# Two phased K pairs instead of four in the second chunk pair, and rests made by adding transfers

## The chip, the cores and the metric

The kernel runs on one core of a Trainium2 chip, as one program. Its time is the device time in microseconds. The core has five engines that run their own streams of instructions and wait for one another by semaphores: TensorE (PE, matrix products), VectorE (DVE), ScalarE (ACT), GpSimd (POOL) and SyncE (SP), which here only issues transfers.

## What is computed

Two layers of a residual trunk over 256 tokens of width 2048, in float32. The change is in the first product of each layer, `proj = h @ w_in`, whose 6144 columns are the queries, keys and values of two groups of eight heads:

```python
def hybrid_mixer(h, layer, w_in, w_o, ...):
    proj = h @ w_in                       # 256 x 2048 @ 2048 x 6144
    q_sb, k_sb, v_sb, q_d, k_d, v_d = jnp.split(proj, offs.tolist(), axis=-1)
    ...                                   # two kinds of attention, eight heads each
    return mix @ w_o

def reference(x, w_in, w_o, ...):
    for l in range(DEPTH):                # DEPTH = 2
        h = rms_norm(x, pre_mix_norm[l])
        m = hybrid_mixer(h, l, w_in[l], w_o[l], ...)
        x = x + rms_norm(m, post_mix_norm[l])
        h = rms_norm(x, pre_ffn_norm[l])
        f = swiglu(h, w_gate[l], w_up[l], w_down[l])
        x = x + rms_norm(f, post_ffn_norm[l])
    return x
```

## The kernel before

**Products.** Float32 is reached with three matmuls on rounded operands: every operand is split into a rounded part `hi` (type fp32r) and a rest `lo` = value − hi, and `product` issues hi·hi, hi·lo and lo·hi into one bank (L1287, L1288, L1289 in the profile; the middle one reads the weights' `lo`). One matmul takes 128 tokens, 128 rows of K and 512 columns.

**Chunk pairs and K pairs.** The twelve chunks of 512 columns are worked on two at a time, in the six chunk pairs of `PAIRS` (n = 0 to 5; n = 1 is called the second pair here). Each has four banks, two token halves by two chunks. K, 2048, is cut into eight K pairs of 2 × 128 rows, so one K pair of one chunk pair is a product of 2 × 2 blocks.

- *Plain* K pairs (`eight_in`, eight products, 24 matmuls) use two tiles of weights, one for each chunk, 128 × 1024 elements or 512 KB each. For one tile SP loads `raw`, ACT copies it to `hi` (L431), and DVE makes `lo` = raw − hi (`rest_of`, L369).
- *Phased* K pairs (`phased`, seven products, 21 matmuls) follow the Strassen-Winograd scheme, with the products g0, t1, t2, t3 in a first part and g1, b22, t4 in a second. They need sums of weights, made by DVE in `first_part` (L378, L380, L384) and `second_part` (L399), with hi and lo of each; and sums of the token side ("forms", `pair_forms` and `token_sums`, the tiles `fin`, `sin`, `shin`, `slin`), made once for each phased K pair (`sums_of`, in the first chunk pair) and used by all later ones. Between the parts the four banks are copied to `w` and combined (L1253 to L1255), and `settle` adds them at the end (L1266).

In n = 0 all eight K pairs are plain. In the others, the K pairs 0 to 3 (`IN_SEVEN`) are phased and come first (the phased half), and 4 to 7 (`IN_PLAIN`) are plain and come behind (the plain half, with eight tiles, numbered 0 to 7 here). `sums_ahead` lets POOL's queue prepare the sums of the next pair's "first" tiles in DRAM during a pair, with a copying transfer (L302) and an adding one (L308).

**Order.** `weight_order` lists all tiles in the order of use, with the roles of those of the phased halves; `queue_phase` adds one phased half. `fetch` issues loads along this list, as the four `raw` buffers come free; `feed_jobs` makes hi and lo, four jobs ahead of the product that asks (`LOOKAHEAD`). hi and lo have six buffers each. Each engine's sequence of instructions is fixed when the program is built, by a scheduler that goes by estimated times, and need not be that of the code.

Tiles have names with their number in the list (`hi57` is the rounded part of tile 57); a second number behind it counts the jobs of a phased tile, and the last is only a running number.

Of the kernel before, what the change touches and what calls it, by code (L numbers as in the profile page):

```python
# [22 lines left out]
KT = D // P  # L23
# [15 lines left out]
IN_SEVEN = (0, 1, 2, 3)  # L39
IN_PLAIN = (4, 5, 6, 7)  # L40
SEVEN = (2, 4, 5, 6)
# [39 lines left out]
def weight_order():  # L81
# [22 lines left out]
    for l in range(L):  # L104
        lay = {"in": {}, "o": {}, "gate": {}, "up": {}, "down": {}}
        for n, (ca, cb) in enumerate(PAIRS):
            if n:
                queue_phase(("in", l, n), "w_in", l, IN_SEVEN, (ca, cb))
            for kp in IN_PLAIN if n else range(KT // 2):
                lay["in"][ca, kp] = queue_pair("w_in", l, kp, ca)  # L110
                lay["in"][cb, kp] = queue_pair("w_in", l, kp, cb)
        queue_phase(("o", l), "w_o", l, KP_O[:2], (0, 1))
        order_o = [(c, kp) for kp in KP_O[2:] for c in (0, 1)]
# [72 lines left out]
def kernel(  # L186
# [48 lines left out]
    for i in range(len(order)):  # L235
        parts = {"u1": 0, "first": 2, "g1": 3}[roles[i][0]] if i in roles else 1
        jobs += [(i, n) for n in range(parts)]
        jobs_to.append(len(jobs))
# [175 lines left out]
    def feed_jobs(upto):  # L414
        while fed[0] < min(upto, len(jobs)):
# [4 lines left out]
            if i in roles:  # L420
                role, key, kps = roles[i]
                if role == "first":
                    first_part(i, n, key, kps[0])
                else:
                    second_part(i, n, key, kps)
                continue
# [562 lines left out]
    def opening(pool, accs, xT, stats, sums_of, settle):  # L989
# [47 lines left out]
        for kp in range(KT // 2):  # L1037
# [10 lines left out]
            if 3 <= kp < 7:  # L1048
                next(stats)
            if 3 <= kp < 3 + len(IN_SEVEN):  # L1050
                sums_of(IN_SEVEN[kp - 3])
# [38 lines left out]
    def mixer_in(pool, l, rs, xT, mix, mixed, began):  # L1090
# [7 lines left out]
        for n, cc in enumerate(PAIRS):  # L1098
# [55 lines left out]
            else:  # L1154
                kps = IN_PLAIN if n else range(KT // 2)
                ahead = list(KP_O[:2]) if alone else []
# [4 lines left out]
                if n:  # L1161
                    open_sums[0] = True
                    w = pool.tile([P, 4, CW], F32, tag="gpost", bufs=1, name=f"w{l}_{n}")
                    w = [w[:, i, :] for i in range(4)]
                    phased(banks, forms, xT, ("in", l, n), IN_SEVEN, w)
                for j, kp in enumerate(kps):
                    last = j == len(kps) - 1
                    if n == 0 and 2 <= j < 2 + len(IN_SEVEN):
                        sums_of(IN_SEVEN[j - 2])
                    if n == 0 and 3 <= j < 7:  # L1170
                        put_away(f"in{l}", j - 3)
# [644 lines left out]
```

## Time and profile before

| what | value |
|---|---|
| median of 3 runs (lowest to highest) | 2188.01 us (2187.4 to 2188.73) |
| the profiled execution | 2187.7 us |
| its span on the core | 2186.0 us |
| granted TensorE clock | 0.999 |
| HBM read and written | 481.12 MB and 29.36 MB |
| transfers issued by POOL: T (gate and up weights) and sum | 122 and 80, of 256 KB each |

The span is the time from the first to the last instruction of the profiled execution; the rest of its time lies around it. In the lines of the profile, "L369 DVE ... x492 | busy, mean ns | idle before" is one group of instructions on one line of the code; a stretch is given as from:to, its length, and then each engine's busy time with the number of its instructions. The input projection, with the attention that runs beside it, takes from 6 us to 304 us in layer 0 and begins at 1090 us in layer 1.

### The profile page before, as it was taken

Reading aid. Unit: us, or ns where it says so; the run is one execution under the profiler, and the core shown is the slowest. Engines: PE = TensorE matmul, PEld = TensorE weight load, DVE = VectorE, ACT = ScalarE, POOL = GpSimd, SP = SyncE. Lnnn points to the kernel's source line nnn. Section 1 sums busy time; section 2 is a strip of 40 time slices with the busy share of each in tenths; the row PEclk is TensorE's granted clock in tenths of the full one; section 3 lists DMA queues with packets and bytes.
Section 4 is the critical chain, followed back from the end, with each engine's and each line's share of the span. In section 5 each row is a group of like instructions: output and inputs, shape, how many; then the busy total and the mean of one; then the engine's idle time right before and its main releaser. Section 6 shows DMA issues by size and latency. Waiting matters only on the chain.

```text
span 2186.0 us, 29154 instructions
## 1 busy us (share of the span) xinstructions
PE 2160.5 (99%) x9872; PEld 1769.3 (81%) x9872; DVE 2013.7 (92%) x2784; ACT 1459.2 (67%) x2203; POOL 310.2 (14%) x318
## 2 busy tenths in 40 slices
PE   9999999999999999999999999999999999999998
PEld 7777888888888888888877778888888888888886
DVE  8998988899999999999898999878999999999997
ACT  7677876656666666666576777757666666676664
POOL 1321000022222220000023110000312212200000
PEclk9999999999999999999999999999999999999999
DMA  8667655587887776767477675655977878767673
GB/s 311 217 206 228 192 210 198 166 298 236 242 258 229 234 237 222 236 222 257 147 257 219 206 230 181 223 198 164 303 237 243 260 223 235 237 216 242 206 266 101
DMA packets 156743, 491.44 MB, mean 225 GB/s; under 512 B 18208, under 2 KB 19232, under 8 KB 155440
## 3 DMA queue, kind: packets, MB, share of 16 engines
q1 hardware_dynamic: 131376, 436.04, 56.7%
q0 software_dynamic: 24640, 53.00, 13.3%
q8 instruction: 77, 1.26, 0.2%
q14 instruction: 74, 0.61, 0.1%
q10 hardware_dynamic: 576, 0.54, 0.1%
HBM read 481.12 MB, written 29.36 MB: 234 GB/s over the span
## 4 chain that ended last, share of the span: by engine, by line
PE 83%; DVE 10%; DMA 3%; ACT 2%; issue 2%; SPq 0%; DVEq 0%; ACTq 0%
PE c L1345 21%; DVE lo L369 5%; PE dn L1665 4%; PE dn L1664 4%; PE dn L1667 4%; PE in L1288 4%; PE in L1287 4%; PE in L1289 4%; PE p L1288 3%; PE c L1288 3%; PE c L1287 3%; PE p L1289 3%; PE c L1289 3%; PE p L1287 3%; PE o L719 2%; PE o L717 2%
## 5 line engine op out<-in xcount | busy, mean ns | idle before, releaser
L369 DVE TENSOR_TENSOR lo<-raw,hi 128x1024 fp32r<-128x1024 f32 (+1 forms) x492 | 580.3, 1195 | 45.7 <-ACT hi L431 38.9
L431 ACT ACTIVATE hi<-raw 128x1024 fp32r<-128x1024 f32 x424 | 436.4, 1058 | 95.2 <-DMA raw<-in_weights_in_turn_dram 58.8
L1345 PE MATMUL c<-hi,xF 128*128 128x512 f32 x1344 | 364.5, 392 | 0.5 <-DVE xF L632 0.5
L1345 PEld LDWEIGHTS c<-hi,xF 128*128 128x128 f32 x1344 | 249.8, 188 | 53.0 <-ACT act L1551 1.4
L324 POOL DMA_DIRECT2D T<-in_weights_in_turn_dram x122 | 107.7, 882 | 1148.5 <-PE c L1345 319.1
L1345 PE MATMUL c<-lo,xF 128*128 128x512 f32 x672 | 207.4, 390 | 0.0
L345 ACT ACTIVATE Th<-T 128x512 fp32r<-128x512 f32 x122 | 77.2, 633 | 192.4 <-DVE T L356 191.3
L345 ACT ACTIVATE Th<-G 128x1024 fp32r<-128x1024 f32 x122 | 129.1, 1058 | 81.1 <-DVE G L357 80.0
L1664 PE MATMUL dn<-hi,jh 128*128 128x512 f32 x416 | 162.0, 389 | 0.0
L1665 PE MATMUL dn<-lo,jh 128*128 128x512 f32 x416 | 161.8, 389 | 0.0
L347 DVE TENSOR_TENSOR Tl<-G,Th 128x1024 fp32r<-128x1024 f32 x122 | 149.1, 1222 | 11.6 <-ACT Th L345 11.6
L347 DVE TENSOR_TENSOR lo<-T,hi 128x1024 fp32r<-128x1024 f32 x122 | 153.9, 1262 | 0.1
L357 DVE TENSOR_TENSOR G<-G,T 128x1024 f32<-128x1024 f32 x122 | 148.8, 1220 | 4.9 <-POOL lo L434 2.7
L431 ACT ACTIVATE hi<-G 128x1024 fp32r<-128x1024 f32 x122 | 129.0, 1057 | 36.3 <-DMA G<-in_weights_in_turn_dram 19.6
L1345 PEld LDWEIGHTS c<-lo,xF 128*128 128x128 f32 x672 | 126.0, 188 | 26.4
L345 ACT ACTIVATE hi<-T 128x1024 fp32r<-128x1024 f32 x122 | 128.1, 1050 | 12.4 <-PE c L1289 9.5
L369 DVE TENSOR_TENSOR lo<-G,hi 128x1024 fp32r<-128x1024 f32 x104 | 126.9, 1220 | 9.3 <-ACT hi L431 9.3
L1667 PE MATMUL dn<-hi,jl 128*128 128x512 f32 x416 | 128.1, 389 | 0.0
L1287 PE MATMUL in<-hi,xT 128*128 128x512 f32 x284 | 112.7, 402 | 0.7 <-ACT hi L1031 0.4
L1288 PE MATMUL in<-lo,xT 128*128 128x512 f32 x284 | 111.4, 393 | 0.2
L1289 PE MATMUL in<-hi,xT 128*128 128x512 f32 x284 | 111.0, 391 | 0.0
L1288 PE MATMUL in<-lo,xI 128*128 128x512 f32 x260 | 102.4, 394 | 4.0 <-DVE lo L369 4.0
(470 smaller groups left out, 5257.6 us busy)
## 6 DMA issues: line engine op xcount, KB each, us to landing
raw<-in_weights_in_turn_dram SPq DMA_DIRECT2D x468, 512.0 KB, 4.8
T<-in_weights_in_turn_dram SPq DMA_DIRECT2D x122, 512.0 KB, 5.1
G<-in_weights_in_turn_dram SPq DMA_DIRECT2D x122, 512.0 KB, 5.4
T<-in_weights_in_turn_dram POOLq DMA_DIRECT2D x122, 256.0 KB, 5.7
sum<-in_weights_in_turn_dram POOLq DMA_DIRECT2D x80, 256.0 KB, 5.0
u<-in_weights_in_turn_dram SPq DMA_DIRECT2D x44, 256.0 KB, 6.0
raw<-in_weights_in_turn_dram SPq DMA_DIRECT2D x34, 256.0 KB, 4.2
raw<-sum SPq DMA_DIRECT2D x30, 256.0 KB, 4.6
```

What stands on the lines that cost most here:

```text
L345: nc.scalar.activation(h, w, AF.Copy)
L347: newest_rest[i] = nc.vector.tensor_tensor(out=l, in0=w, in1=h.bitcast(F32), op=ALU.subtract)
L357: nc.vector.tensor_tensor(out=g, in0=g, in1=t2.unsqueeze(1).to_broadcast([P, 2, CW]), op=ALU.add)
L369: rests.append(nc.vector.tensor_tensor(out=lo, in0=src, in1=hi.bitcast(F32), op=ALU.subtract))
L431: nc.scalar.activation(hi, raw, AF.Copy)
L1287: nc.tensor.matmul(a, sh, hi, start=first, stop=False, skip_group_check=open_sums[0])
L1288: nc.tensor.matmul(a, sh, lo, start=False, stop=False, skip_group_check=open_sums[0])
L1289: newest_product[0] = nc.tensor.matmul(a, sl, hi, start=False, stop=last, skip_group_check=open_sums[0])
L1345: nc.tensor.matmul(a, stat[part], w[j][:, kk, :], start=first and kk + n == 0, stop=last and kk == 1 and n == 2)
L1664: nc.tensor.matmul(accs[c, t], sh, hi[:, kk, :], start=first, stop=False, skip_group_check=open_sums[0])
L1665: nc.tensor.matmul(accs[c, t], sh, lo[:, kk, :], start=False, stop=False, skip_group_check=open_sums[0])
L1667: nc.tensor.matmul(accs[c, t], sl, hi[:, kk, :], start=False, stop=last, skip_group_check=open_sums[0])
```

## The change

1. The second pair (n = 1) has two phased K pairs, 0 and 1, and six plain ones. The others are as before. The forms of K pairs 2 and 3, first read in the third pair now, are made in the code of the plain half of n = 1 (`FORMS_AT`: ahead of its plain K pairs number 1 and 3) and no longer in that of n = 0.
2. In the plain halves of n = 2 to 5, in both layers, tiles 2, 4 and 6 (`BY_TRANSFER`) get their rest in another way. ACT writes `hi`, then writes −hi into `lo` (the same copy with scale −1), and a transfer on POOL's queue reads the tile from DRAM once more and adds it to `lo`. DVE has no part in it, and `raw` is free once ACT has read it twice.

```diff
--- before.py
+++ after.py
@@ -37,7 +37,10 @@
 O_SEVEN = (4, 5)
 PAIRS = ((6, 8), (10, 7), (9, 0), (11, 2), (1, 3), (4, 5))
 IN_SEVEN = (0, 1, 2, 3)
-IN_PLAIN = (4, 5, 6, 7)
+IN_SEVENS = ((), (0, 1), IN_SEVEN, IN_SEVEN, IN_SEVEN, IN_SEVEN)
+IN_PLAIN = tuple(tuple(kp for kp in range(8) if kp not in mine) for mine in IN_SEVENS)
+FORMS_AT = {(1, 1): 2, (1, 3): 3}
+BY_TRANSFER = (2, 4, 6)
 SEVEN = (2, 4, 5, 6)
 FIRST_SEVEN = (6,)
 FIRST_ORDER = (0, 1, 3, 2, 7, 4, 6, 5)
@@ -105,10 +108,13 @@
         lay = {"in": {}, "o": {}, "gate": {}, "up": {}, "down": {}}
         for n, (ca, cb) in enumerate(PAIRS):
             if n:
-                queue_phase(("in", l, n), "w_in", l, IN_SEVEN, (ca, cb))
-            for kp in IN_PLAIN if n else range(KT // 2):
+                queue_phase(("in", l, n), "w_in", l, IN_SEVENS[n], (ca, cb))
+            first = len(order)
+            for kp in IN_PLAIN[n]:
                 lay["in"][ca, kp] = queue_pair("w_in", l, kp, ca)
                 lay["in"][cb, kp] = queue_pair("w_in", l, kp, cb)
+            if len(IN_SEVENS[n]) > 2:
+                roles.update({first + j: ("transfer", ("in", l, n), ()) for j in BY_TRANSFER})
         queue_phase(("o", l), "w_o", l, KP_O[:2], (0, 1))
         order_o = [(c, kp) for kp in KP_O[2:] for c in (0, 1)]
         order_o += [(c, kp) for kp in LATE_O for c in (2, 3)] + [(c, kp) for c in (2, 3) for kp in LAST_O]
@@ -233,7 +239,7 @@
     jobs = []
     jobs_to = []
     for i in range(len(order)):
-        parts = {"u1": 0, "first": 2, "g1": 3}[roles[i][0]] if i in roles else 1
+        parts = {"u1": 0, "first": 2, "g1": 3, "transfer": 1}[roles[i][0]] if i in roles else 1
         jobs += [(i, n) for n in range(parts)]
         jobs_to.append(len(jobs))
 
@@ -419,7 +425,12 @@
             fed[0] += 1
             if i in roles:
                 role, key, kps = roles[i]
-                if role == "first":
+                if role == "transfer":
+                    hi, lo = ready[i] = split_tile(i)
+                    nc.scalar.activation(hi, raw, AF.Copy)
+                    nc.scalar.activation(lo, raw, AF.Copy, scale=-1.0)
+                    nc.gpsimd.dma_start(lo, stream[i].bitcast(F32R), accum_op=ALU.add)
+                elif role == "first":
                     first_part(i, n, key, kps[0])
                 else:
                     second_part(i, n, key, kps)
@@ -1047,7 +1058,7 @@
                     settle(part[0])
             if 3 <= kp < 7:
                 next(stats)
-            if 3 <= kp < 3 + len(IN_SEVEN):
+            if 3 <= kp < 5:
                 sums_of(IN_SEVEN[kp - 3])
 
     def first_stats(pool, rs):
@@ -1152,7 +1163,7 @@
                 opening(pool, banks, xT, first_stats(pool, rs), sums_of, settle)
                 start(lambdas())
             else:
-                kps = IN_PLAIN if n else range(KT // 2)
+                kps = IN_PLAIN[n]
                 ahead = list(KP_O[:2]) if alone else []
                 if n + 1 < len(PAIRS):
                     start(sums_ahead(("in", l, n + 1)))
@@ -1162,11 +1173,13 @@
                     open_sums[0] = True
                     w = pool.tile([P, 4, CW], F32, tag="gpost", bufs=1, name=f"w{l}_{n}")
                     w = [w[:, i, :] for i in range(4)]
-                    phased(banks, forms, xT, ("in", l, n), IN_SEVEN, w)
+                    phased(banks, forms, xT, ("in", l, n), IN_SEVENS[n], w)
                 for j, kp in enumerate(kps):
                     last = j == len(kps) - 1
-                    if n == 0 and 2 <= j < 2 + len(IN_SEVEN):
+                    if n == 0 and 2 <= j < 4:
                         sums_of(IN_SEVEN[j - 2])
+                    if (n, j) in FORMS_AT:
+                        sums_of(FORMS_AT[n, j])
                     if n == 0 and 3 <= j < 7:
                         put_away(f"in{l}", j - 3)
                     if n == 0 and j < 3:
```

Over the whole program PE has 9690 matmuls (9678 before), DVE 2232 tensor_tensor instructions (2281), ACT 1851 activations (1837), POOL issues 223 transfers (203) and SP 904 (907). The lines behind the new ones have moved: L369 is L375 now, L431 is L442, L302 and L308 are L308 and L314, L378 to L399 are L384 to L405, L1253 is L1266, L1266 is L1279, L1295 is L1308; the new instructions are L430 (hi), L431 (−hi) and L432 (the adding transfer).

**ACT, layer 0, plain half of the fourth pair** (chunks 11 and 2; tiles 56 to 63 are its tiles 0 to 7). Before:

```order
L431 ACTIVATE hi56_1781<-raw56_1779 128x1024
L431 ACTIVATE hi57_1796<-raw57_1794 128x1024
L431 ACTIVATE hi58_1805<-raw58_1803 128x1024
L431 ACTIVATE hi59_1817<-raw59_1815 128x1024
L431 ACTIVATE hi60_1833<-raw60_1831 128x1024
L431 ACTIVATE hi61_1842<-raw61_1840 128x1024
```

After:

```order
L442 ACTIVATE hi56_1764<-raw56_1762 128x1024
L442 ACTIVATE hi57_1779<-raw57_1777 128x1024
L430 ACTIVATE hi58_1788<-raw58_1786 128x1024
L442 ACTIVATE hi59_1801<-raw59_1799 128x1024
L431 ACTIVATE lo58_1789<-raw58_1786 128x1024
L430 ACTIVATE hi60_1817<-raw60_1815 128x1024
L431 ACTIVATE lo60_1818<-raw60_1815 128x1024
L442 ACTIVATE hi61_1827<-raw61_1825 128x1024
```

The copy into `lo58` (tile 2) does not follow `hi58` but stands behind `hi59`, which is made from the next tile's load; `lo60` (tile 4) follows `hi60` directly. In the third pair, and in both layers, the copy of tile 2 stands in the same place.

**POOL, the same place** (sum65 to sum69 belong to the phased half of the fifth pair, sum81 to that of the sixth). Before:

```order
L302 DMA sum68_1695<-in_weights_in_turn_dram 16x4096
L302 DMA sum69_1732<-in_weights_in_turn_dram 16x4096
L308 DMA sum65_1640<-in_weights_in_turn_dram 128x512
L308 DMA sum66_1662<-in_weights_in_turn_dram 128x512
L308 DMA sum68_1695<-in_weights_in_turn_dram 128x512
L308 DMA sum69_1732<-in_weights_in_turn_dram 128x512
L302 DMA sum81_2064<-in_weights_in_turn_dram 16x4096
```

After:

```order
L308 DMA sum69_1715<-in_weights_in_turn_dram 16x4096
L314 DMA sum65_1623<-in_weights_in_turn_dram 128x512
L314 DMA sum66_1645<-in_weights_in_turn_dram 128x512
L314 DMA sum68_1688<-in_weights_in_turn_dram 128x512
L432 DMA lo58_1789<-in_weights_in_turn_dram 128x1024
L432 DMA lo60_1818<-in_weights_in_turn_dram 128x1024
L314 DMA sum69_1715<-in_weights_in_turn_dram 128x512
L432 DMA lo62_1860<-in_weights_in_turn_dram 128x1024
L308 DMA sum81_2050<-in_weights_in_turn_dram 16x4096
```

The three transfers into `lo` stand between the adding ones for the sums, and that of `sum69` stands behind those of `lo58` and `lo60`.

**DVE, phased half of the second pair** (chunks 10 and 7). Layer 0, from the 90th instruction to the 97th, before:

```order
L369 TENSOR_TENSOR lo18_1_644<-u1_16_1_618,hi18_1_643 128x512
L378 TENSOR_TENSOR raw20_654<-raw20_654 128x512
L369 TENSOR_TENSOR lo18_1_644<-raw18_635,hi18_1_643 128x512
L380 TENSOR_TENSOR u1_19_0_650<-u1_19_0_650,raw20_654 128x512
L369 TENSOR_TENSOR lo20_0_657<-raw20_654,hi20_0_656 128x1024
L369 TENSOR_TENSOR lo20_1_663<-u1_19_0_650,hi20_1_662 128x512
L384 TENSOR_TENSOR raw20_654<-raw20_654,u1_19_0_650 128x512
L378 TENSOR_TENSOR first21_682<-first21_682 128x512
```

After, the same numbers:

```order
L375 TENSOR_TENSOR lo18_1_620<-u1_16_1_594,hi18_1_619 128x512
L405 TENSOR_TENSOR u1_16_0_592<-raw19_626,u1_16_0_592 128x512
L375 TENSOR_TENSOR lo18_1_620<-raw18_611,hi18_1_619 128x512
L405 TENSOR_TENSOR u1_16_1_594<-raw19_626,u1_16_1_594 128x512
L375 TENSOR_TENSOR lo19_0_629<-raw19_626,hi19_0_628 128x1024
L375 TENSOR_TENSOR lo19_1_635<-u1_16_0_592,hi19_1_634 128x1024
L1266 TENSOR_TENSOR w0_1_591<-w0_1_591 128x512
L375 TENSOR_TENSOR lo19_2_652<-u1_16_1_594,hi19_2_651 128x1024
```

From the 71st to the 90th the two orders have the same rows. Where the sums and rests of the third "first" tile (20) and the fourth (21) stood, those of the g1 tile (19) come. Layer 1, behind the same two first tiles (409 and 410), before:

```order
L369 TENSOR_TENSOR lo410_1_10645<-raw410_10636,hi410_1_10644 128x512
L380 TENSOR_TENSOR u1_411_1_10716<-u1_411_1_10716,first413_10741 128x512
L369 TENSOR_TENSOR lo412_0_10722<-raw412_10718,hi412_0_10721 128x1024
L369 TENSOR_TENSOR lo412_1_10727<-u1_411_0_10714,hi412_1_10726 128x512
L384 TENSOR_TENSOR raw412_10718<-raw412_10718,u1_411_0_10714 128x512
L369 TENSOR_TENSOR lo413_0_10745<-first413_10741,hi413_0_10744 128x1024
L369 TENSOR_TENSOR lo412_1_10727<-raw412_10718,hi412_1_10726 128x512
L384 TENSOR_TENSOR first413_10741<-first413_10741,u1_411_1_10716 128x512
```

After:

```order
L375 TENSOR_TENSOR lo410_1_10609<-raw410_10600,hi410_1_10608 128x512
L1310 TENSOR_TENSOR sin1_2_10812<-fin1_2_10809 128x128
L1311 TENSOR_TENSOR sin1_2_10812<-fin1_2_10809,sin1_2_10812 128x128
L1098 TENSOR_TENSOR fin1_3_10897<-xI0_6_9979 128x256
L1098 TENSOR_TENSOR fin1_3_10897<-xI0_7_9980 128x256
L1310 TENSOR_TENSOR sin1_3_10900<-fin1_3_10897 128x128
L1308 TENSOR_TENSOR sin1_3_10900<-fin1_3_10897 128x128
L1309 TENSOR_TENSOR sin1_3_10900<-sin1_3_10900,fin1_3_10897 128x128
L1311 TENSOR_TENSOR sin1_3_10900<-fin1_3_10897,sin1_3_10900 128x128
L375 TENSOR_TENSOR lo411_0_10679<-raw411_10676,hi411_0_10678 128x1024
L375 TENSOR_TENSOR lo411_1_10685<-u1_408_0_10557,hi411_1_10684 128x1024
L375 TENSOR_TENSOR lo411_2_10697<-u1_408_1_10559,hi411_2_10696 128x1024
```

The forms of K pairs 2 and 3 (`sin1_2`, `fin1_3`, `sin1_3`), which stood ahead of this half, now stand in it, ahead of the rests of the g1 tile (411). In layer 0 the rows of these forms stay among those of the first pair.

## The prediction

> **What bounds the kernel.** I read the page first (busy times, the chain that ended last, groups, DMA), then PE's waits, then the stretches of the input projection, then the timelines around the tiles that the change touches.
>
> ```profile
> PE 2160.5 (99%) x9872; PEld 1769.3 (81%) x9872; DVE 2013.7 (92%) x2784; ACT 1459.2 (67%) x2203; POOL 310.2 (14%) x318
> ...
> PE 83%; DVE 10%; DMA 3%; ACT 2%; issue 2%; SPq 0%; DVEq 0%; ACTq 0%
> ...
> L369 DVE TENSOR_TENSOR lo<-raw,hi 128x1024 fp32r<-128x1024 f32 (+1 forms) x492 | 580.3, 1195 | 45.7 <-ACT hi L431 38.9
> ```
>
> PE bounds the whole, and a tenth of the chain is DVE. ACT has a third of the span free and a copy of a tile costs it 1.06 us (rows in part d); a rest costs DVE about 1.2 us. So work moved from DVE to ACT pays only where DVE holds PE up. That is read by stretch: the phased halves of the second pair (layers 0 and 1, first two rows), of the third (next two) and of the fifth (next two), and the plain half of the fourth (last).
>
> ```profile
> core 0: us, PE busy (x) PEld busy (x) DVE busy (x) ACT busy (x) POOL busy (x), PEclk, DMA share, GB/s
> 50.57:76.83 26.26, 24.67 (x107) 17.65 (x106) 26.26 (x31) 19.39 (x28) 15.31 (x21) 1.00 0.79 244
> 1138.10:1163.40 25.30, 21.15 (x91) 15.85 (x90) 25.30 (x30) 18.35 (x25) 17.84 (x24) 1.00 0.67 200
> 100.15:123.22 23.07, 21.87 (x100) 16.82 (x99) 23.05 (x40) 20.84 (x47) 16.16 (x16) 1.00 0.65 190
> 1187.80:1212.80 25.00, 22.74 (x97) 16.74 (x96) 24.80 (x43) 21.88 (x48) 9.53 (x16) 1.00 0.71 199
> 198.73:226.90 28.17, 26.42 (x132) 20.34 (x132) 28.10 (x50) 26.59 (x56) 5.48 (x8) 1.00 0.69 196
> 1286.90:1313.40 26.50, 25.64 (x131) 20.49 (x130) 26.43 (x47) 25.27 (x53) 5.38 (x8) 1.00 0.74 208
> 174.50:198.73 24.23, 24.23 (x121) 19.57 (x120) 18.09 (x23) 12.32 (x23) 0.00 (x0) 1.00 0.74 254
> ```
>
> In the phased halves DVE has no free moment (26.26 of 26.26, 25.30 of 25.30) while PE stands still in between. In the plain half of the fourth pair PE never stops (24.23 of 24.23) and DVE has 6.14 us free: the rests that the change takes from DVE stand where DVE is not short. The clock is 1.00 throughout and plays no part.
>
> **(a) Twelve more matmuls.** One K pair of one chunk pair takes 24 matmuls plain and 21 phased; two K pairs in two layers are 2 × 2 × 3 = 12 more. Their price:
>
> ```profile
> 179.67 0.39 PE L1288 MATMUL in<-lo,xT 128*128 128x512 f32 x1
> ...
> 180.35 0.39 PE L1288 MATMUL in<-lo,xT 128*128 128x512 f32 x1
> 180.58 0.39 PE L1289 MATMUL in<-hi,xT 128*128 128x512 f32 x1
> ```
>
> The first and the last row stand four starts apart: 0.91 / 4 = 0.227 us. PE is the bound, so 12 × 0.227 = **+2.7 us** in full.
>
> **(b) The second pair, two phased K pairs fewer.** Four phased K pairs are 84 matmuls, 84 × 0.227 = 19.1 us; the stretch takes 26.26 us in layer 0 and 25.30 in layer 1. The other matmuls in it (107 − 84 = 23, and 7) are mostly transposes of some 0.1 us (below, seven in 0.93), so 1.8 and 0.7 us. About 5.4 us are lost to DVE in each layer.
>
> ```profile
> 56.36 1.34 DVE L369 TENSOR_TENSOR lo<-raw,hi 128x1024 fp32r<-128x1024 f32 x1
> ...
> 60.47 0.93 PE L1138 MATMUL qkT_ps<-ident,tok 128*128 128x128 f32 x7
> ...
> PE in L1288 <- DVE lo L369: 7.2, 10, 1.4
> ```
>
> Layer 0: with two K pairs DVE still has the same rows to do up to the 90th, then two additions and the rest of the g1 tile, in the place and of the size of the third first tile's, which ended at 56.36 + 1.34 = 57.7. PE, which began at 50.57 and has 8 products of 3 matmuls to do first, is there at 50.57 + 24 × 0.227 = 56.0 and waits some 1.5 us; waits of about 0.5 us on the two next rests follow, 2.4 us of loss for 5.4. Gain 3.
>
> Layer 1: the first rows wait for a load, and eleven small rows of the forms now stand in the half as well, eight of 0.2 us from start to start and three of 0.37:
>
> ```profile
> 1128.44 0.75 DVE L1087 TENSOR_TENSOR fin<-xI 128x256 f32<-128x256 f32 x2
> 1129.11 0.28 DVE L1297 TENSOR_TENSOR sin<-fin 128x128 f32<-128x128 f32 x1
> 1129.31 0.68 DVE L1306 TENSOR_TENSOR slin<-sin,shin 128x512 fp32r<-128x512 f32 x1
> ...
> 1133.94 0.69 DVE L380 TENSOR_TENSOR u<-u,raw 128x512 f32<-128x512 f32 x1 [0.47 <-DMA raw<-sum]
> ```
>
> From 1133.94 it is seven rows of 0.6 us, one rest of 1.2, the forms' 2.7 and the g1 rest of 1.3: done at 1143.3, where PE comes at 1138.10 + 5.45 = 1143.55. Some 1 us of waits stays for the slower DVE rows that this stretch has; gain 4.5. Together **−7.5 us**; the ends are 0 (all the loss moves to the plain half) and −10.8 (all of it goes). I stay between, by the rows above.
>
> **(c) The third pair's phased half.** DVE reaches it with less left over, but its work there stays, and the additions that close the second pair wait for PE's last product:
>
> ```profile
> 100.74 1.26 DVE w L1266 x2
> ```
>
> These come after 100.15 whatever DVE had done before. I take 1 us in each layer, **−2**; ends 0 and −4.4 (PE's idle time in the two stretches is 1.20 and 2.26, the rest hidden in short gaps).
>
> **(d) Twenty-four rests by transfer.** For tiles 2, 4 and 6 of each plain half, ACT writes hi, then lo = −hi (1.06 us), and then POOL's queue adds the 512 KB tile from DRAM onto lo. No such transfer of 512 KB stands in the trace. Its neighbours:
>
> ```profile
> raw<-in_weights_in_turn_dram SPq DMA_DIRECT2D x468, 512.0 KB, 4.8
> T<-in_weights_in_turn_dram POOLq DMA_DIRECT2D x122, 256.0 KB, 5.7
> sum<-in_weights_in_turn_dram POOLq DMA_DIRECT2D x80, 256.0 KB, 5.0
> ...
> DMA to landing us min/median/max: 2.6/5.1/11.3
> ...
> q0 software_dynamic: 24640, 53.00, 13.3%
> ```
>
> An accumulating 256 KB lands in 5.0 to 5.7 us, say 5.4. The second 256 KB costs what POOL's queue takes for a byte: 13.3% × 2186 / 53.00 = 5.49 us of all 16 engines for one MB, 1.4 us for 0.262 MB. So **landing L = 6.8 us**. Ends: 2.6 + 1.4 = 4.0 (the fastest row) and 11.3 (the slowest). The Trainium skill, page "DMA: Bandwidth & Descriptors", section "Anatomy of one DMA — SWDGE (gpsimd) path", fits a transfer on this queue by 2.0 us and its bytes at 436 GB/s, which makes 3.2 us here; the trace disagrees, since for 256 KB the fit gives 2.6 and the medians are 5.0 and 5.7. By the fit (d) would be some 6 us.
>
> What counts is when the copy −hi is made. In ACT's new order it stands behind the hi of the next tile, and that waits for its own load. ACT's rows before (fourth pair layer 0, with tile 4's hi behind it, third layer 0, fourth layer 1, third layer 1, then fifth and sixth of layer 0), the load that tile 3 of the first waits for, and PE's first use of tile 2's lo in the same order (the first is 180.35, above):
>
> ```profile
> 177.80 1.06 ACT L431 ACTIVATE hi<-raw 128x1024 fp32r<-128x1024 f32 x1 [5.27 <-DMA raw<-in_weights_in_turn_dram]
> 180.04 1.06 ACT L431 ACTIVATE hi<-raw 128x1024 fp32r<-128x1024 f32 x1 [1.19 <-DMA raw<-in_weights_in_turn_dram]
> 126.70 1.06 ACT L431 ACTIVATE hi<-raw 128x1024 fp32r<-128x1024 f32 x1 [3.61 <-DMA raw<-in_weights_in_turn_dram]
> 1266.22 1.06 ACT L431 ACTIVATE hi<-raw 128x1024 fp32r<-128x1024 f32 x1 [5.48 <-DMA raw<-in_weights_in_turn_dram]
> 1214.21 1.06 ACT L431 ACTIVATE hi<-raw 128x1024 fp32r<-128x1024 f32 x1 [1.77 <-DMA raw<-in_weights_in_turn_dram]
> 224.47 1.16 ACT L431 ACTIVATE hi<-raw 128x1024 fp32r<-128x1024 f32 x1
> 277.33 2.02 ACT L431 ACTIVATE hi<-raw 128x1024 fp32r<-128x1024 f32 x2
> ```
>
> ```profile
> 169.10 0.33 SPq L284 DMA_DIRECT2D raw<-in_weights_in_turn_dram  x1
> ```
>
> ```profile
> 132.93 0.39 PE L1288 MATMUL in<-lo,xT 128*128 128x512 f32 x1
> 1268.57 0.39 PE L1288 MATMUL in<-lo,xI 128*128 128x512 f32 x1
> 1222.39 0.39 PE L1288 MATMUL in<-lo,xI 128*128 128x512 f32 x1
> 234.82 0.40 PE L1288 MATMUL in<-lo,xT 128*128 128x512 f32 x1
> 286.17 0.40 PE L1288 MATMUL in<-lo,xT 128*128 128x512 f32 x1
> ```
>
> hi's start + 1.06 for hi + 1.06 for the copy + 6.8, against the use: fourth pair, layer 0: 177.80 + 2.12 + 6.8 = 186.72 against 180.35, a wait of 6.4 us; layer 1: 1275.14 against 1268.57, 6.6; third pair, layer 0: 135.62 against 132.93, 2.7; layer 1: 1223.13 against 1222.39, 0.7. Fifth pair: 224.47 + 1.16 + 1.06 + 6.8 = 233.5 against 234.82, and sixth: 277.33 + 2.02 + 6.8 = 286.15 against 286.17: nothing, and I take the same for layer 1. Sum **+16.4 us**; with L = 4.0 it would be 7.3, with 11.3 over 40.
>
> Tiles 4 and 6 cost nothing more, under cover of tile 2's wait: in the fourth pair ACT's hi of tile 4 began at 180.04 and its transfer would land at about 189, where PE, 5.45 us of K pair and 6.4 of wait behind 180.35, comes at 192. Without that wait tile 4 itself would cost 3 us. Tile 6's load comes some 3.4 us later, since its raw buffer is now let go by ACT's copy and not by DVE; it has the same cover and one K pair more. On POOL's queue one accumulation for the next pair's sums stands behind the transfer of tile 4; the fifth pair begins at 198.73, more than 10 us later, so it costs nothing. Taking the rests off DVE in the plain halves itself gains nothing there (24.23 of 24.23).
>
> **(e) What is given back.** The fifth pair's phased half leaves PE idle for 28.17 − 26.42 = 1.75 us and 0.86 us, with DVE full. DVE, freed and with PE held up, comes to it ahead; half of it, **−1.3**.
>
> The forms of K pairs 2 and 3 are first read in the third pair. In layer 0 the order leaves their rows among those of the first pair; in layer 1 they are counted in (b). Beyond that, nothing.
>
> Sum: 2.7 − 7.5 − 2 + 16.4 − 1.3 = **+8.3**. The profiled execution took 2187.7 us (span 2186.0), so 2196.0; the median of the runs, 2188.01, lies 0.3 higher: **2196.3 us**. Less than 0.2% (4.4 us) I count as no change, about what this kernel's timing can tell.
>
> **The rivals.** *Faster: the copy comes ahead of the use.* If the load of tile 3 lands early, ACT's copy −hi does too, and no transfer is waited for. Place: the fourth pair, where that load, issued at 169.10, was still awaited at 177.80, 8.7 us against a median of 4.8. For: DVE is freed earlier and lets raw buffers go earlier. Against: the loads share their engines with POOL's transfers, and there are now more of these. hi would have to end by 172.5 for all of the wait to go, and some 4 us sooner than now in each layer for the whole to come out even. With no wait left it is 2.7 − 7.5 − 2 = −6.8: 2181.2 us.
>
> *No change: a quick landing.* With L = 4.0 the waits are 7.3 us and the sum 2.7 − 7.5 − 2 + 7.3 − 1.3 = −0.8: 2187.2; up to L = 5.7 it stays within 0.2%. For: the fastest accumulation took 2.6. Against: both medians. The Trainium skill's fit (page and section above) would bring the time here, to some 2186.
>
> *Slower, no relief.* (b), (c) come to nothing, because the DVE work of the plain tiles fills the freed time: 2.7 + 16.4 − 1.3 = +17.8: 2205.8. For: DVE is full in these stretches. Against: plain tiles take one DVE instruction each.
>
> *Slower, crowded engines.* The plain halves keep the DMA engines 0.74 busy already and get 3 × 0.524 × 5.49 = 8.6 us of all 16 more. If landings reach 9.5 us the waits are 31 and the sum is +23: 2211 and more.
>
> **Chances.** Forecast 0.44; faster rival 0.17; quick landing 0.18; no relief 0.16; crowded engines 0.05. So faster 0.17, same 0.18, slower 0.65. The range 2181 to 2212 takes in all cases but the crowded one; the forecast's own, with L from 5.7 to 8, is 2192 to 2203.
>
> **What would show it.** PE waiting for a DMA into lo at the matmul that reads tile 2's lo (L1288 of before) in the fourth pair for 6 us in each layer, and 1 to 3 in the third; POOL's 512 KB transfers landing in 6 to 8 us; the second pair's phased half with waits of 1 to 2.5 us, not 5.4. I am wrong if no wait on lo's transfer shows, or if the copy −hi runs well before PE's use; or if the loads of raw tiles, not the rests, become what PE waits for.

## The result, and the profile after

The changed kernel takes 2244.3 us (median of 4 runs, 2240.17 to 2246.14), the kernel before 2187.7 beside it: a ratio of 1.0261 with a 95% interval of 1.0249 to 1.0274, 57 us slower. The forecast was 2196.3 us, with a range of 2181 to 2212. The direction was right, the size was not: the loss is almost seven times the forecast one.

The page of the changed kernel, then the landing times of transfers (KB each, median us from issue to landing); the last row is that of the kernel before, for its sum loads:

```profile
PE 2177.3 (97%) x9884; PEld 1782.5 (79%) x9884; DVE 1974.1 (88%) x2735; ACT 1471.8 (66%) x2217; POOL 327.3 (15%) x338
...
q0 software_dynamic: 27744, 64.53, 15.5%
...
PE 78%; DVE 9%; DMA 6%; issue 3%; ACT 3%; SPq 0%; DVEq 0%; ACTq 0%; POOLq 0%
...
T<-in_weights_in_turn_dram POOLq DMA_DIRECT2D x122, 256.0 KB, 5.8
sum<-in_weights_in_turn_dram POOLq DMA_DIRECT2D x76, 256.0 KB, 5.1
lo<-in_weights_in_turn_dram POOLq DMA_DIRECT2D x24, 512.0 KB, 8.7
raw<-sum SPq DMA_DIRECT2D x30, 256.0 KB, 10.7
```

```profile
raw<-sum SPq DMA_DIRECT2D x30, 256.0 KB, 4.6
```

DVE did what the change says: 39.6 us less work. PE has 16.8 us more of it, though the twelve added matmuls are 2.7 of that, and it stands still for 67 us of its span where it stood for 26. The chain now holds DMA for 6%, twice as much. A transfer into lo lands after 8.7 us, not 6.8; and SP's loads from the prepared sums, which the change does not touch, take 10.7 us in place of 4.6.

What PE waited for, and what DVE waited for, in all (us in total, times, longest):

```profile
PE in L1301 <- DMA lo<-in_weights_in_turn_dram: 27.3, 8, 7.1
PE o_sb L861 <- ACT v L1125: 6.2, 2, 3.1
PE in L1300 <- ACT v L1125: 6.2, 2, 4.9
...
DVE u L386 <- DMA raw<-sum: 83.9, 19, 9.3
```

```profile
DVE u L380 <- DMA raw<-sum: 9.8, 9, 3.0
```

The second fence is the kernel before. So three things are new: waits for lo (27.3 us, eight of them, one in each changed pair and layer), waits for ACT's copy v of a finished bank (12.4 us), and DVE standing 84 us for the sum loads where it stood 10.

The fourth pair of layer 0 shows the first of them, and something that had no place in the forecast. Stretches before, in and behind the wait, whose last three numbers are the granted clock, the DMA engines' busy share and GB/s; then PE, ACT and POOL in order of time:

```profile
core 0: us, PE busy (x) PEld busy (x) DVE busy (x) ACT busy (x) POOL busy (x), PEclk, DMA share, GB/s
179.00:186.60 7.60, 7.60 (x35) 6.31 (x34) 3.39 (x3) 3.71 (x4) 0.91 (x1) 1.00 0.79 242
186.60:194.00 7.40, 0.42 (x2) 0.00 (x0) 2.45 (x2) 4.20 (x5) 1.75 (x2) 0.84 0.97 238
194.00:198.10 4.10, 3.94 (x9) 3.14 (x10) 0.12 (x1) 0.00 (x0) 0.90 (x1) 0.50 1.07 248
198.10:202.00 3.90, 3.90 (x21) 3.14 (x20) 0.57 (x1) 1.30 (x2) 0.00 (x0) 0.96 1.07 266
```

```profile
186.41 0.61 PE L1300 MATMUL in<-hi,xT 128*128 128x512 f32 x2
194.16 0.79 PE L1301 MATMUL in<-lo,xT 128*128 128x512 f32 x1 [7.13 <-DMA lo<-in_weights_in_turn_dram]
194.75 0.63 PE L1302 MATMUL in<-hi,xT 128*128 128x512 f32 x1
195.17 0.63 PE L1301 MATMUL in<-lo,xT 128*128 128x512 f32 x1
...
177.54 1.07 ACT L430 ACTIVATE hi<-raw 128x1024 fp32r<-128x1024 f32 x1
182.89 1.06 ACT L442 ACTIVATE hi<-raw 128x1024 fp32r<-128x1024 f32 x1 [4.28 <-DMA raw<-in_weights_in_turn_dram]
183.85 1.04 ACT L431 ACTIVATE lo<-raw 128x1024 fp32r<-128x1024 f32 x1
...
185.34 0.91 POOL L432 DMA_DIRECT2D lo<-in_weights_in_turn_dram  x1 [12.03 <-DVE lo L375]
```

ACT's copy −hi could have run at 178.6 and runs at 183.85, behind the next tile's hi, which waits for its load: that is the order that the prediction read. The transfer is issued at 185.34, 0.44 us behind the copy's end, and PE goes on at 194.16. Then PE runs at half speed: the starts are 0.42 us apart, the granted clock is 0.50 for some four microseconds, and nine matmuls take what eighteen took. The Trainium skill, page "TensorE: Matmul & The Clock Gate", section "Part 1: The HAM clock gate (the "warmup" mystery)", says that the array's clock halves after an idle window of about 3.4 us and comes back after as long a busy one. The trace agrees with the two states, 0.50 here and 1.00 in all stretches shown of before, but not with the 3.4 us: waits of 3.1 us, and two of 1.3 and 0.6 us close together, were enough here. Over the whole execution 67 matmuls of 512 columns start 0.42 to 0.44 us behind the one before and not the usual 0.227 (13.4 us lost); in the kernel before there are 10 (2.0 us).

Stage by stage, from first matmul to first matmul of the next pair (for the sixth pair, to its own last matmul), by PE's timeline:

| stage | layer 0: before, after | layer 1: before, after | both, difference |
|---|---|---|---|
| second pair, with the step behind it | 49.6, 49.4 | 49.7, 51.6 | +1.7 |
| third | 53.4, 59.9 | 53.9, 60.5 | +13.1 |
| fourth | 45.2, 53.9 | 45.2, 56.0 | +19.5 |
| fifth | 56.9, 61.1 | 55.2, 60.2 | +9.2 |
| sixth | 48.0, 50.2 | 48.0, 49.7 | +3.9 |
| all behind the sixth | 786.6, 791.2 | 795.9, 801.5 | +10.2 |

With the two first pairs (+0.8) that makes 58.4, the difference of the two spans. Behind the sixth pair nothing was changed, and yet 10 us are lost there.

In the third to sixth pairs the whole loss of 45.7 us lies in the plain halves (+47.2). The phased halves, where DVE is short, are 1.5 us shorter in all. Those of the third pair (layers 0 and 1) and of the fifth after the change, in the columns above; before they took 23.07, 25.00, 28.17 and 26.50 us (the prediction shows these stretches):

```profile
100.59:125.40 24.81, 23.59 (x99) 18.30 (x99) 24.58 (x42) 21.85 (x48) 9.37 (x16) 0.93 0.75 201
1216.53:1241.41 24.88, 24.40 (x99) 18.77 (x99) 24.65 (x42) 21.85 (x48) 9.25 (x16) 0.88 0.72 198
214.40:240.38 25.98, 25.62 (x132) 20.55 (x130) 25.91 (x47) 24.61 (x45) 5.40 (x8) 1.00 0.74 212
1332.98:1358.52 25.54, 25.43 (x131) 20.55 (x130) 25.50 (x46) 24.41 (x43) 5.38 (x8) 1.00 0.76 216
```

All 19 of DVE's waits for the sum loads fall among plain K pairs too, where DVE has time to spare, so only part of their 84 us can reach PE. One way is the copy v, below. PE's waits for the attention that runs beside grow as well, from 3.8 to 9.1 us (at `za_sb`, `o_df` and `pT_df`); that DVE's standing is behind these is not shown.

The second pair itself does what was forecast. From its first matmul to its last it takes 47.7 and 46.4 us where it took 49.4 and 49.5, 4.8 us less in the two layers together; the forecast was −7.5 + 2.7 = −4.8. It loses this at the step to the third pair, which takes 1.7 and 5.3 us from start to start where it took 0.2. PE and ACT there in layer 1:

```profile
1211.26 0.39 PE L1302 MATMUL in<-hi,xI 128*128 128x512 f32 x1
1216.53 0.79 PE L1300 MATMUL in<-hi,xI 128*128 128x512 f32 x1 [4.88 <-ACT v L1125]
...
1215.27 0.63 ACT L392 ACTIVATE hi<-raw 128x512 fp32r<-128x512 f32 x1 [1.98 <-DVE raw L390]
1215.80 0.67 ACT L1125 ACTIVATE v<-in,rs_in 128x512 f32<-128x512 f32 x1
```

The bank could be copied at 1211.7. ACT is held at a hi of the third pair, which waits for DVE's sum, and DVE is late because it has waited for sum loads (6.7, 1.8 and 1.7 us up to 1207.6); v stands behind this hi. In the order before, v stood ahead of this hi.

### The profile page after: what moved, and what is told of

The parts are those of the page before. It is cut to its first block, busy times and chain, and to the rows that moved or that the text cites. A ratio compares the mean times of both kernels' runs of the same rounds, so it can differ in the third digit from the quotient of the medians.

```text
span 2244.4 us, 29167 instructions
## 1 busy us (share of the span) xinstructions
PE 2177.3 (97%) x9884; PEld 1782.5 (79%) x9884; DVE 1974.1 (88%) x2735; ACT 1471.8 (66%) x2217; POOL 327.3 (15%) x338
## 4 chain that ended last, share of the span: by engine, by line
PE 78%; DVE 9%; DMA 6%; issue 3%; ACT 3%; SPq 0%; DVEq 0%; ACTq 0%; POOLq 0%
PE c L1358 19%; DVE lo L375 5%; PE dn L1680 4%; PE dn L1678 4%; PE dn L1677 4%; PE in L1301 3%; PE in L1302 3%; PE in L1300 3%; PE p L1301 3%; PE c L1300 3%; PE c L1301 3%; PE p L1302 3%; PE c L1302 3%; PE p L1300 3%; DMA raw<-sum 2%
## 5 line engine op out<-in xcount | busy, mean ns | idle before, releaser
L375 DVE TENSOR_TENSOR lo<-raw,hi 128x1024 fp32r<-128x1024 f32 (+1 forms) x470 | 557.7, 1201 | 68.0 <-ACT hi L442 65.0
L442 ACT ACTIVATE hi<-raw 128x1024 fp32r<-128x1024 f32 x408 | 419.4, 1057 | 100.3 <-DMA raw<-in_weights_in_turn_dram 76.1
L442 ACT ACTIVATE hi<-G 128x1024 fp32r<-128x1024 f32 x122 | 128.8, 1056 | 35.7 <-DMA G<-in_weights_in_turn_dram 21.8
L375 DVE TENSOR_TENSOR lo<-G,hi 128x1024 fp32r<-128x1024 f32 x104 | 127.1, 1222 | 9.1 <-ACT hi L442 9.1
L1301 PE MATMUL in<-lo,xT 128*128 128x512 f32 x294 | 117.8, 401 | 15.5 <-DMA lo<-in_weights_in_turn_dram 14.5
L1301 PE MATMUL in<-lo,xI 128*128 128x512 f32 x270 | 108.5, 402 | 13.7 <-DMA lo<-in_weights_in_turn_dram 12.8
L1300 PE MATMUL in<-hi,xT 128*128 128x512 f32 x294 | 118.0, 406 | 1.7 <-ACT v L1125 1.3
L1302 PE MATMUL in<-hi,xT 128*128 128x512 f32 x294 | 116.8, 398 | 0.0
```

The lines of the kernel that those rows point to most:

```text
L375: rests.append(nc.vector.tensor_tensor(out=lo, in0=src, in1=hi.bitcast(F32), op=ALU.subtract))
L442: nc.scalar.activation(hi, raw, AF.Copy)
L1300: nc.tensor.matmul(a, sh, hi, start=first, stop=False, skip_group_check=open_sums[0])
L1301: nc.tensor.matmul(a, sh, lo, start=False, stop=False, skip_group_check=open_sums[0])
L1302: newest_product[0] = nc.tensor.matmul(a, sl, hi, start=False, stop=last, skip_group_check=open_sums[0])
```

## The experiments

All changes are against the kernel before unless a line says otherwise; ratios are to the kernel before, run beside.

**The second pair's change alone** (e1). `BY_TRANSFER = ()`.

> The second pair's change alone, no transfers. Theory 'order' (in ACT's order the copy of the first bank, v, now stands behind a hi that waits for a late sum load, so PE waits at the step to the third pair and then runs at half clock): the second pair itself gains 4.8 us as forecast, the step loses about 11.8 (1.5 + 5.0 of wait, 2.2 + 3.1 of slow clock in the changed kernel's trace), so some 7 us slower than before, near 2194. Rival 'as forecast' (the wait at the step was a consequence of the transfers): 4.8 us faster, near 2183, no wait on v.

Measured: 2187.65 us, ratio 1.0005 (0.9996 to 1.0014). No change: the gain is there (the second pair takes 47.0 and 47.9 us, 4.0 less) and is given back at the step (1.4 and 4.6 us, before 0.2).

```profile
PE in L1300 <- ACT v L1125: 5.2, 2, 4.2
...
1170.98 0.69 DVE L386 TENSOR_TENSOR u<-u,raw 128x512 f32<-128x512 f32 x1 [7.09 <-DMA raw<-sum]
```

The wait for v stands here without any transfer into lo, so it belongs to the second pair's change; the rival falls. The expected loss of 11.8 us, waits and slow clock together, was too much: the step is 5.5 us longer, and slow matmuls behind it show in layer 1 alone, some 2 us.

**The same with v ahead** (e5). The last plain K pair of the second pair feeds three jobs ahead and not four for its first token half, and the next hi is put behind v in order:

```diff
+ with tc.issue_after(first_v[0]) if j and first_v[0] is not None else nullcontext():
      nc.scalar.activation(hi[:, j, :], src, AF.Copy)
```

> As the second pair's change alone, but ACT's copy v of the second pair's first bank is put ahead of the hi that waits for a load. Theory 'order': the wait on v goes and most of the 11.8 us come back, 2183 to 2187, at or below before. Rival 'late sums' (the third pair's own weights come late, and the wait only changes its name): the same time as with the second pair's change alone, with PE waiting for lo or hi in its place.

Measured: 2187.01 us, 1.0001 (0.9992 to 1.001). The wait for v is 0.5 us, and another stands in its place, for the additions that close the pair, which are DVE's:

```profile
PE in L1307 <- DVE w L1286: 4.5, 2, 2.8
```

So ACT's order was the place of the wait, not its cause, and the time is that of e1: the rival holds, though PE waits for the closing additions and not for lo or hi. DVE is late, and the wait that the trace shows ahead of it is for the third pair's sum loads (16.8 us for such loads in the whole execution, before 9.8).

**The transfers alone** (e2). `IN_SEVENS = ((), IN_SEVEN, ...)`, forms as before.

> The transfers alone, four phased K pairs in the second pair. If the two parts are independent: the 58 us of the changed kernel less the 7 of the second pair's change, about +51, near 2239. Waits on lo's transfers of 25 to 29 us in eight places as in the changed kernel. If the second part's loss needs the first part's: under +40.

Measured: 2243.24 us, 1.0255 (1.0241 to 1.0269). The whole loss, and the two parts do not need each other. PE waits 26.5 us for lo, DVE 61.8 for the sum loads, and the loads from the sums take 9.6 us.

**Sixth pair only** (e4). `if n == 5:` at the roles of the transfers.

> Transfers in the sixth pair only (six in all), nothing else changed. Theory 'direct' (the loss is PE's wait for the transfers into lo): 1.4 + 1.0 us as in the changed kernel, no half clock behind such short ones: +2.4, near 2190. Theory 'crowding' (the transfers make the sum loads of the output projection late, then DVE, then ACT's copy v, and PE waits for that and runs slowly after): also the 10.2 us that the changed kernel lost behind the sixth pair: +12 to +14, near 2201.

Measured: 2198.88 us, 1.0055 (1.0041 to 1.0068), +12: "crowding". PE, whole execution, and DVE, layer 0 from 280 to 310 us:

```profile
PE o_sb L861 <- ACT v L1125: 6.2, 2, 3.1
PE in L1301 <- DMA lo<-in_weights_in_turn_dram: 1.2, 2, 0.7
...
DVE u L386 <- DMA raw<-sum: 8.2, 2, 6.2
```

PE's direct wait is 1.2 us of 12; the sixth pairs are 3.1 us longer, and 9.0 are lost behind them. In each layer the transfers make two loads late that belong to the output projection, DVE waits 8.2 us for them (in the same stretch of before no such wait shows), and ACT's v and with it PE come late. SP issued these loads at 282.28 and 284.44 us, before at 283.75 and 284.85, and they landed 9.4 and 11.1 us later, before 3.9 and 5.0: they aren't issued late, they take longer.

**Copying, not adding** (e6), against e2: `nc.gpsimd.dma_start(lo, stream[i].bitcast(F32R))` without `accum_op`.

> The transfers alone (four phased K pairs in the second pair), but the 24 transfers copy the tile into lo and do not add it: the addition is left out, lo then holds the whole tile. Same bytes, same queue, same places. Theory 'adding' (the addition makes a transfer slow, 8.7 us, and holds the DMA engines so that the loads of the sums come late): landing about 5 us, the loads of raw from the sums back from 9.6 to about 5 us, waits for lo under 10 us in all, total +5 to +12. Rival 'bytes' (12.6 MB more to move in a busy stretch are the cost, whatever is done with them): landing still 7 us and more, loads from the sums 8 us and more, total above +35.

Measured: 2207.04 us, 1.0093 (1.0076 to 1.011), +19, between the two; PE waits 12.3 us for lo. e2 first, then e6:

```profile
q0 software_dynamic: 28096, 65.58, 15.8%
lo<-in_weights_in_turn_dram POOLq DMA_DIRECT2D x24, 512.0 KB, 8.7
raw<-sum SPq DMA_DIRECT2D x30, 256.0 KB, 9.6
```

```profile
q0 software_dynamic: 28096, 65.58, 14.7%
lo<-in_weights_in_turn_dram POOLq DMA_DIRECT2D x24, 512.0 KB, 6.5
raw<-sum SPq DMA_DIRECT2D x30, 256.0 KB, 6.5
```

The same packets and bytes. Against the 13.3% and 53.00 MB of before, the 12.58 MB of added transfers take 15.8% × 2241.8 − 290.7 = 63.5 us of all 16 engines when they add and 14.7% × 2204.1 − 290.7 = 33.3 when they copy: 5.0 against 2.6 us for a MB. Adding is some 36 of the 56 us. But copying is not free.

**The copy −hi in place** (e7), against e2: the next tile's hi is put behind it.

```diff
- nc.scalar.activation(lo, raw, AF.Copy, scale=-1.0)
+ neg_copy[0] = nc.scalar.activation(lo, raw, AF.Copy, scale=-1.0).ins
...
+ with tc.issue_after(neg_copy[0]) if neg_copy[0] is not None else nullcontext():
      nc.scalar.activation(hi, raw, AF.Copy)
```

> The transfers alone, with ACT's copy -hi straight behind the hi of its own tile (it stood behind the next tile's hi for tile 2 in the third to fifth pair). If both causes hold: the transfers start up to 5 us earlier, the waits for lo fall from 26.5 us to 5 to 12 and the slow clock behind them goes (some 10 us), the late sum loads stay (median 9 us): total +25 to +33 where the transfers alone had +55. If ACT's order were the whole cause: under +8. If it were none of it: +50 and more.

Measured: 2234.89 us, 1.0219 (1.0202 to 1.0236), +47. A miss: the waits for lo fell by 17 us, to 9.7, as expected, but the total by 9 only. DVE still waits 42.0 us for sum loads, and the fifth pair became longer (63.8 us in layer 0, 60.2 in e2). What was taken out of one wait came back in another.

**One tile of the three** (e8, e9, e13), against e2: `BY_TRANSFER = (2,)`, `(6,)` and `(4,)`.

> The transfers alone, tile 2 of each plain half only (8 in all). Theory 'two causes' (tile 2 carries PE's waits for lo; tiles 4 and 6, which run while the sums of the next phased half are loaded, carry the late loads): waits for lo 18 to 26 us with slow clock behind them, loads from the sums back to about 5 us, no wait for v behind the sixth pair: +25 to +38. Rival (every transfer does the same harm, 55/24 = 2.3 us): +18, with a third of the late loads.

> The transfers alone, tile 6 of each plain half only (8 in all). Theory 'two causes': waits for lo under 3 us; loads from the sums late (median 6 us and more), the waits for v behind the sixth pair of about 6 us in all: +8 to +18. Rival 'every transfer the same': +18 with waits for lo. Rival 'only a pile of transfers crowds': no change within 4 us, loads from the sums at 5 us.

> The transfers alone, tile 4 of each plain half only (8 in all). If the losses of the three tiles add up, 55 - 30 - 13 = +12. If tile 4 does harm only in a pile with the others: within 5 us of before. Waits for lo of 1 to 6 us, since the cover of tile 2's wait is gone (the prediction said 3 us for the fourth pair).

Measured: tile 2 alone 2218.46 us, 1.0143 (1.0123 to 1.0163), +30; tile 4 alone 2206.14, 1.0093 (1.0078 to 1.0108), +20; tile 6 alone 2200.82, 1.006 (1.0042 to 1.0078), +13. Waits of PE for lo, in this order (tile 6 has none), and DVE's for the sum loads:

```profile
PE in L1301 <- DMA lo<-in_weights_in_turn_dram: 25.6, 8, 8.2
DVE u L386 <- DMA raw<-sum: 5.7, 7, 1.8
```

```profile
PE in L1301 <- DMA lo<-in_weights_in_turn_dram: 7.6, 3, 4.2
DVE u L386 <- DMA raw<-sum: 25.7, 16, 4.2
```

```profile
DVE u L386 <- DMA raw<-sum: 24.8, 14, 4.4
```

So the two harms belong to different tiles. Tile 2 is waited for, and DVE waits no longer for the sums than before (their loads land after 5.9 us, before 4.6). Tiles 4 and 6 run while the next half's sums are loaded and make DVE wait for these. With tile 4 alone PE waits for it, 4.2 and 2.9 us in the fourth pairs, near the 3 us that the prediction gave for the case without tile 2's cover. The three add up to 63, a little more than the 56 of all. That is not so place by place: behind the sixth pair, where the changed kernel lost 10.2 us, each tile alone costs at most some 2 us, so that loss needs the transfers together. On tile 6 two things that were expected did not come: a late median of the sum loads (it is 5.0 us; only some of them were late), and waits for v behind the sixth pair (PE's 4.0 us for v lie at the steps between the pairs).

**Both remedies** (e14), and **no transfers at all** (e15 with the copy in place, e16 in the order of the changed kernel): e7 with a copying transfer; e7 and e2 without the line of the transfer.

> Both remedies on the transfers alone: ACT's copy -hi straight behind its hi, and the 24 transfers copy the tile and do not add it (the addition is left out, lo holds the whole tile). Theory 'two causes, ACT's order and the slow addition': almost all goes, 0 to +7 us against before, waits for lo under 3 us. Rival 'a third cause' (more bytes, POOL's queue, ACT's second copy, raw buffers let go later): the order alone gave back only 9 of 55 us, so +10 to +15 stay.

> The transfers alone with the copy in place, but the 24 transfers are left out (lo stays at -hi): ACT's second copies and the work taken from DVE are there, the bytes are not. What is left of the 16 us that neither the order nor the addition explained: if it is the transfers' bytes and POOL's queue, this is back at before, -5 to +3 us; if it is ACT's second copy, the later release of the raw buffers or the new order of the engines, +10 to +16 stay.

> The transfers alone in ACT's order of the changed kernel, with the 24 transfers left out (lo stays at -hi). With no landing to wait for, a late copy costs PE little (the copies of tile 2 end 0.4 us ahead of their use or more). Bytes theory: -6 to +3 us. If ACT's order and copies cost by themselves: +10 and more.

Measured: e14 2202.85 us, 1.0079 (1.006 to 1.0097), +16; e15 2185.96, 0.9999 (0.9989 to 1.001); e16 2187.78, 1.0006 (0.9996 to 1.0015). "Two causes" falls in e14, where 16 us stay with PE waiting only 2.9 us for lo; and in e15 and e16 they are gone. So the rest belongs to the transfers themselves; these runs don't part their bytes from their place on POOL's queue. DVE's 24 spared rests, ACT's 24 further copies, the raw buffers let go later and the other order of the engines come to nothing in sum, with either order, within some 2 us; what each is worth by itself is not shown. In e15 the sum loads are as quick as ever:

```profile
raw<-sum SPq DMA_DIRECT2D x30, 256.0 KB, 4.1
```

**Earlier sums** (e10, and e11 with v ahead), against e1 and e5: in layer 1 `start(sums_ahead(("in", l, 2)), 12)` in the first pair.

> The second pair's change alone, and in layer 1 the sums of the third pair are made during the first pair and not during the second. Theory 'late sums' (the first sum load of the third pair takes 9.7 us because it lies among eight adding transfers, DVE waits 7.1 us for it, and the copy v behind it 4.2): the wait for v in layer 1 and the slow clock behind it go, 6 to 7 us faster than the second pair's change alone, 2178 to 2182 and so faster than before by over 0.2%. Rival 'buffers' (the loads are late because the raw buffers come free late): no change against the second pair's change alone, 2186 to 2188, DVE still waits 7 us.

> The same with ACT's copy v put ahead as in the run before. By 'late sums' the additions that close the second pair are no longer late in layer 1, so putting v ahead does no harm and may help layer 0 by some 1 us: 2177 to 2181. By 'buffers': 2186 to 2188.

Measured: 2185.2 us, 0.9996 (0.9988 to 1.0005), and 2185.21, 0.9993 (0.9985 to 1.0002). "Late sums" falls: the last of the adding transfers was issued at 1144 us, the first sum load at 1166, and DVE still waited, 5.9 us at a stretch, for a sum load (layer 1, 1130 to 1190 us of e10):

```profile
DVE u L386 <- DMA raw<-sum: 8.0, 2, 5.9
```

This load did land sooner, 6.2 us after its issue where in e1 it took 9.6. But it was issued at 1166.2 us and not at 1161.3, and what the landing won, the issue lost. SP's queue waited there for DVE's rests, which let raw buffers go (24.3 us from 1140 to 1175 us). That fits "buffers", but no run tried it by itself, so the cause stays open. None of these versions beats the kernel before beyond its interval.

## Why the prediction was right and wrong

- **(a) and (b), the second pair: right in size, wrong in what follows.** −4.8 us were forecast and −4.8 measured inside the pair (−4.0 in e1). The step that failed is that nothing was counted at the step to the third pair, which takes 6.5 us more. There v stands behind a hi that waits for DVE, one place later in order than before; with v put ahead (e5), PE waits for DVE's closing additions in its place.
- **(c), the third pair's phased half: wrong in sign.** Forecast −2, measured +1.6 (24.8 and 24.9 us, before 23.1 and 25.0). In e1, without transfers, it takes 24.8 and 24.8, so this belongs to the second pair's change.
- **(d), the transfers: the mechanism right, the term mis-sized.** The late copy is there, and the four waits that were worked out as 6.4, 6.6, 2.7 and 0.7 us came as 7.1, 7.1, 3.8 and 4.3; four more of 0.5 to 2.4 us came in the fifth and sixth pairs, where nothing was forecast. Forecast 16.4, measured 27.3. L was 8.7 us, not 6.8. One reason is a row that was read wrongly: the 80 transfers of `sum` are 40 that copy and 40 that add. Landing times before, of the copying ones (L302), the adding ones (L308) and the adding ones into T (L324):

```profile
DMA to landing us min/median/max: 2.6/3.1/6.8
DMA to landing us min/median/max: 3.9/7.2/11.3
DMA to landing us min/median/max: 3.5/5.7/8.8
```

So 5.0 was the median of a mixture, and the "fastest accumulation" of 2.6 us, on which the rival "quick landing" rests, was a copy; the fastest that added took 3.5. Adding transfers of 256 KB took 5.7 and 7.2 us. The second 256 KB then cost 1.5 to 3.0 us, for which 1.4 was taken. That 1.4 is their time if all 16 engines are free for them (5.0 us for a MB measured, 5.49 taken), and in the stretch of the wait the engines were 0.97 busy with SP's loads as well. With L = 8.7 the same sum would have given 26.4, or 28.9 with the fifth and sixth pairs of layer 1 taken as in layer 0, as the prediction says (it leaves them out in its 31 for L = 9.5 too, which would be 35). That this is near 27.3 is in part luck: in three of the four places the copy ended 1.7 to 2.1 us earlier ahead of PE's use than forecast, and some 0.4 us from the copy to the transfer's issue were not counted.
- **Costed at nothing: the loads beside the transfers.** The prediction counted the transfers' engine time (8.6 us of all 16 in a plain half) in one rival and gave it 0.05, and in that rival let it act only on the landing. It acts on the loads for the next half as well: the sum loads took 10.7 us, not 4.6, DVE stood 84 us for them, and v came late; 10.2 us were lost behind the sixth pair alone. "More than 10 us later, so it costs nothing" was said of the sums' accumulation on POOL's queue; the loads behind it on SP's queue were not counted. This is what it is worth: with tile 2 alone, waits and slow clock together cost 30 us, and with these for its 16.4 the prediction's sum would be +22, still inside its range. The other 26 us of e2's loss belong to tiles 4 and 6 and take it out. So do the 8 us that (a), (b), (c) and (e) were to give together: in e1 they come to nothing.
- **"The clock is 1.00 throughout and plays no part": wrong.** It held before, where PE's longest wait in the projection was 1.4 us. The change made PE stop for 3 to 7 us at a time, and the slow matmuls behind such waits cost 11 us more in all.
- **(e): right in sign, its cause not shown.** The fifth pair's phased halves are 3.2 us shorter, where 1.3 was forecast. But they are 2.6 shorter in e1, with no transfer and no rest taken off DVE. The +9.2 of the two fifth pairs lies in their plain halves (+12.4), where PE waits for lo and for steps of the attention that runs beside.
- **Taking the rests off DVE gains nothing in the plain halves: right**, as e15 and e16 show.
- **The rivals.** "No relief" and "quick landing" didn't come. "Crowded engines" came, with waits for lo of 27 us (31 were worked out), and its +23 held less than half of what crowding does.

## What to carry to other kernels

A transfer that takes work from an engine is paid for with DMA engine time: before it is put in a stretch where the engines are 0.74 busy, see what else is loaded there and in the stretch behind, and for which loads an engine in order would stand still. An adding transfer costs about twice the engine time of a copying one here, and its landing, in a full stretch, is longer than that engine time. And ask first whether the engine that is relieved is short at that place: here its whole relief was worth 0.

## What the runs showed of the hardware

- On POOL's queue 512 KB landed after 8.7 us when added to what stood in SBUF (medians of 8.3 to 9.0 in seven kernels) and after 6.5 and 6.6 when copied (e6, e14), and took 5.0 against 2.6 us of all 16 DMA engines for a MB (e2, e6). Of 256 KB within DRAM, in the kernel before: 7.2 us when added, 3.1 when copied.
- With all 24 adding transfers, SP's 30 loads of 256 KB from the sums landed after 9.6 and 10.7 us in the median (e2 and the changed kernel) and not after 4.6; with 24 copying ones after 6.5 (e6).
- Behind each of the changed kernel's seven waits of PE of 3.1 us or longer the granted clock was 0.50 for 3 to 6 us, and matmuls of 512 columns started 0.42 us apart and not 0.23. Shorter waits did it at times: two of 1.3 and 0.6 us close together at 101 us did, one of 2.4 at 250 us did not.
